# A two-layer decoder trunk on one core: seven weight pieces per pair of k-tiles from the first pair on, ten begun products in sections, and x's first tile loaded ahead of the weights

## The chip, the cores and the metric

The kernel runs on one core of one Trainium2 chip. The metric is device time in microseconds for one execution, the median of several runs. A core has five engines that run side by side, each through its own list of instructions in order: TensorE (PE in the profile; PEld is its weight load), VectorE (DVE), ScalarE (ACT), GpSimd (POOL) and SyncE (SP). Here SP issues the DMA transfers (SPq).

## The reference, cut to what matters

The trunk has two layers on 256 rows of 2048 values. Layer 0 is a Mamba-2 mixer, layer 1 an attention layer. The change touches layer 0 alone, up to its scan:

```python
shift, scale, gate = split(silu(c) @ ada_w[0] + ada_b[0], 3)
h = x * (1 + scale) + shift                       # 256 x 2048
z, xBC, dt = split(h @ in_w)                      # in_w: 2048 x 10304
xBC = silu(causal_depthwise_conv(xBC) + conv_b)   # -> xs, B, C
y = ssd_scan(xs * softplus(dt), -exp(A_log), B, C) + xs * D
y = rmsnorm_per_group(y * silu(z)) @ out_w
x = layer_norm(alpha * x + (1 + gate) * y)
```

Everything is computed in f32. The input `c` is one vector, so `silu(c) @ ada_w` is a product of a matrix with a vector.

## The kernel before, in words

**Tiles.** The 2048 values of the contraction are 16 k-tiles of 128. The first product `h @ in_w` is cut into 20 blocks of 512 columns: `bc` blocks 0 to 3 (for head groups 0/1, 2/3, 4/5, 6/7; `win[0]` to `win[3]`), `xs` blocks for groups 0 to 7 (`win[4]` to `win[11]`) and `z` blocks for groups 0 to 7 (`win[12]` to `win[19]`). A block needs 8 *pieces*; a piece is the weights of two k-tiles, 128 x 1024 f32 (`raw`, L86). So layer 0's first product is 160 pieces.

**Precision.** Each f32 operand is split into a rounded high half and a rest. ACT writes the high half of a piece (`whi`, L94), DVE the low half (`wlo`, L96), and each product is three matmuls: high with high, high with low, low with high. A piece takes 24 matmuls of 256 columns where it is the stationary operand (`cm_piece`, `bc` and `xs`, L120 to L122) or 12 of 512 where it streams (`tm_piece`, `z`, L173 to L175). There are six buffers for `raw` and three each for `whi` and `wlo`.

**The modulation.** `ada_w[0]` is stored by columns of the output, as 128 x 2048 tiles (`araw`). One DVE instruction multiplies such a tile with `silu(c)`, which stands in every partition (`cb_`), and sums along the row (L239): one *dot product* gives scale or shift of one k-tile. So a k-tile of `h` needs two loads of 1 MB and two dot products, then `ada_bias` (L244), the modulation on ACT (`htmp`, L381), the high half on ACT (`actT`, L382) and the low half on DVE (L383). `h_step` (L366) is one such dot product with what follows; `fetch` (L361) loads the next column, at most four ahead. `xt` holds two k-tiles of the transposed x.

**The first phase** (L354 to L452) runs while `h` comes into being. The two blocks `win[0]` and `win[4]` are computed whole, piece by piece as the k-tiles appear, in PSUM banks of their own. PE would have little to do in that time, so other products are *begun*: the table `begun` (L295) names the block, the k-tile at which its first part ends, and a place in SBUF. The sum up to there is copied from PSUM to that place by ACT (L443). Here eight products are begun, with 34 of their pieces, one product after the other. The list `order` has 50 pieces. In the first two pairs of k-tiles it has four pieces, in the later ones seven, and at the end the small product for `dt` comes with two loads (L411). `fetch_piece` (L398) loads a piece some places ahead of its use.

**Behind it**, `product` (L329) computes each remaining block from its k-tile `k0` on, and adds the part in SBUF, where there is one: on DVE (L340 for `z`, L347 for the others). The group's convolution (DVE, L308) and scan (`stage1`, `stage2`) follow; DVE's share of the scan is L513 to L553. The 16 dot products of layer 0's gate are put in one per five pieces (`background`).

**The order.** The program is written in one order, and a scheduler of the language orders it anew on each engine by its own estimate of when things are ready. Every load goes through SP in order; a load whose buffer is not free yet holds up those behind it.

## Time and profile before

| what | value |
|---|---|
| median of 3 runs | 1313.19 us (1312.98 to 1313.73) |
| the profiled execution | 1312.58 us, its span 1310.8 us |
| PE busy | 1241.7 us (95%) |
| DVE busy | 1027.8 us (78%) |
| ACT busy | 704.7 us (54%) |
| mean DMA rate over the span | 256 GB/s |
| first matmul | 20.6 us |

Read it in stretches, since the share of busy time is a mean over stages with different limits. The first phase ends at about 185 us, the scan of layer 0 at about 540. A matmul's end is modelled, so busy PE time also holds stretches in which PE runs below its best pace; counts of pieces per time tell more.

### The profile page before, as it was taken

What the parts mean: (1) busy time and instruction counts of PE and PEld (TensorE: products, weight loads), DVE (VectorE), ACT (ScalarE), POOL (GpSimd) and SP (SyncE); (2) the same over time, 40 slices, a digit from 0 to 9 for tenths busy, and PEclk for the clock granted to TensorE, in tenths of its full rate; (3) what the DMA queues carried; (4) which work ended last, traced back from release to release, by engine and by line L of the source; (5) the groups of instructions that cost most, each with busy time, mean ns of one, the idle gap of its engine ahead of it and who ended that gap; (6) DMA issues with size and microseconds to landing.
All of it is one profiled execution on the core that took longest, in us unless ns stands there. A gap on an engine that the chain in (4) does not pass through costs nothing.

```text
span 1310.8 us, 19308 instructions
## 1 busy us (share of the span) xinstructions
PE 1241.7 (95%) x7378; PEld 1091.6 (83%) x7378; DVE 1027.8 (78%) x1447; ACT 704.7 (54%) x1028; POOL 26.4 (2%) x20
## 2 busy tenths in 40 slices
PE   3799999999999999999999899999999999999995
PEld 3699988899989899767888699888888888888884
DVE  6889786999996688889765577888787757758677
ACT  3454478757766677864333444444445644444551
POOL 0000000000000000000000043000000000000000
PEclk9999999999999999999999999999999999999998
DMA  9999867777857555388977675899998664363571
GB/s 386 423 422 423 303 218 250 266 265 275 306 200 233 177 192 177 123 294 322 384 258 219 194 225 181 302 406 339 351 391 309 212 187 151 100 191 96 160 273 65
DMA packets 80446, 335.86 MB, mean 256 GB/s; under 512 B 8961, under 2 KB 9057, under 8 KB 67553
## 3 DMA queue, kind: packets, MB, share of 16 engines
q1 hardware_dynamic: 80352, 334.62, 71.8%
q8 instruction: 58, 0.95, 0.3%
q14 instruction: 36, 0.29, 0.1%
HBM read 332.41 MB, written 2.18 MB: 255 GB/s over the span
## 4 chain that ended last, share of the span: by engine, by line
PE 77%; DVE 10%; DMA 6%; ACT 4%; issue 3%; SPq 0%; ACTq 0%; DVEq 0%
PE acc L152 11%; PE acc L174 11%; PE acc L175 11%; PE acc L173 11%; PE acc L122 7%; PE acc L120 7%; PE acc L121 7%; PE acc L153 6%; DMA araw<-in_ada 5%; DVE wlo L96 3%; DVE araw L239 2%; PE py L551 2%; DVE cacc L308 1%; ACT whi L94 1%; PE aux L755 1%
## 5 line engine op out<-in xcount | busy, mean ns | idle before, releaser
L96 DVE TENSOR_TENSOR wlo<-raw,whi 128x1024 fp32r<-128x1024 f32 x394 | 484.5, 1239 | 198.9 <-ACT whi L94 193.1
L94 ACT ACTIVATE whi<-raw 128x1024 fp32r<-128x1024 f32 x394 | 414.5, 1057 | 374.9 <-PE acc L175 174.2
L173 PE MATMUL acc<-whi,actT 128*128 128x512 f32 x704 | 271.6, 394 | 22.8 <-ACT actT L382 20.6
L174 PE MATMUL acc<-wlo,actT 128*128 128x512 f32 x704 | 277.1, 394 | 4.8 <-DVE wlo L96 4.6
L120 PE MATMUL acc<-actT,whi 128*128 128x256 f32 x960 | 272.6, 287 | 6.2 <-ACT whi L94 4.7
L122 PE MATMUL acc<-actT,wlo 128*128 128x256 f32 x960 | 269.8, 286 | 5.1 <-DVE wlo L96 5.0
L121 PE MATMUL acc<-actT,whi 128*128 128x256 f32 x960 | 271.6, 284 | 0.0
L152 PE MATMUL acc<-actT,whi 128*128 128x512 f32 x704 | 250.1, 397 | 0.0
L239 DVE SCALAR_TENSOR_TENSOR araw<-araw,cb__72 128x2048 f32<-128x2048 f32 x96 | 219.3, 2285 | 14.8 <-DMA araw<-in_ada 14.5
L153 PE MATMUL acc<-actT,wlo 128*128 128x256 f32 x704 | 201.3, 286 | 0.9 <-DVE wlo L96 0.9
L120 PEld LDWEIGHTS acc<-actT,whi 128*128 128x128 f32 x960 | 185.6, 194 | 8.3 <-ACT whi L94 5.9
L122 PEld LDWEIGHTS acc<-actT,wlo 128*128 128x128 f32 x960 | 183.6, 193 | 7.2 <-DVE wlo L96 7.2
L121 PEld LDWEIGHTS acc<-actT,whi 128*128 128x128 f32 x960 | 185.6, 193 | 0.4
L175 PE MATMUL acc<-whi,actT 128*128 128x512 f32 x448 | 175.1, 391 | 0.0
L173 PEld LDWEIGHTS acc<-whi,actT 128*128 128x128 f32 x704 | 132.0, 188 | 50.8 <-ACT actT L382 20.6
L174 PEld LDWEIGHTS acc<-wlo,actT 128*128 128x128 f32 x704 | 132.5, 188 | 35.8 <-DVE wlo L96 9.2
L152 PEld LDWEIGHTS acc<-actT,whi 128*128 128x128 f32 x704 | 132.1, 188 | 29.3
L153 PEld LDWEIGHTS acc<-actT,wlo 128*128 128x128 f32 x704 | 133.2, 189 | 2.4 <-DVE wlo L96 1.7
L175 PE MATMUL acc<-whi,ylo 128*128 128x512 f32 x256 | 100.5, 393 | 0.0
L175 PEld LDWEIGHTS acc<-whi,actT 128*128 128x128 f32 x448 | 84.4, 188 | 16.8
L175 PEld LDWEIGHTS acc<-whi,ylo 128*128 128x128 f32 x256 | 48.0, 188 | 9.6
L308 DVE SCALAR_TENSOR_TENSOR cacc<-acc,prm,cacc 128x253 f32<-128x253 f32 (+2 forms) x96 | 42.1, 474 | 7.9 <-ACT cacc L305 7.5
(203 smaller groups left out, 1064.7 us busy)
## 6 DMA issues: line engine op xcount, KB each, us to landing
araw<-in_ada SPq DMA_DIRECT2D x96, 1024.0 KB, 7.6
raw<-in_win SPq DMA_DIRECT2D x160, 512.0 KB, 5.0
raw<-in_wkv SPq DMA_DIRECT2D x72, 512.0 KB, 6.4
raw<-in_wout SPq DMA_DIRECT2D x64, 512.0 KB, 4.7
raw<-in_wbin SPq DMA_DIRECT2D x64, 512.0 KB, 3.6
raw<-in_wk SPq DMA_DIRECT2D x24, 512.0 KB, 8.0
cbc<-cumd SPq DMA_DIRECT2D x16, 512.0 KB, 5.3
raw<-in_wbout SPq DMA_DIRECT2D x16, 512.0 KB, 4.5
```

The costliest lines, as they stand in the source:

```text
L94: S.activation(hi, raw, AF.Copy)
L96: latest[0] = V.tensor_tensor(lo, raw, hi.bitcast(F32), op=ALU.subtract)
L120: T.matmul(o, hi[:, k, c_], ahi[:, kt, :], start=first, stop=False, skip_group_check=True)
L121: T.matmul(o, hi[:, k, c_], alo[:, kt, :], start=False, stop=False, skip_group_check=True)
L122: T.matmul(o, lo[:, k, c_], ahi[:, kt, :], start=False, stop=kt == k1 - 1, skip_group_check=True)
L152: T.matmul(ps[n], hi[:, k, c_], xp[:, kt], start=kt == 0, stop=False, skip_group_check=True)
L153: T.matmul(ps[n][:, 0, :], lo[:, k, c_], xhi[:, kt, :], start=False, stop=kt == KT - 1, skip_group_check=True)
L173: T.matmul(ps[b], h_, hi[:, k, :], start=kt == k0, stop=False)
L174: T.matmul(ps[b], h_, lo[:, k, :], start=False, stop=False)
L175: T.matmul(ps[b], l_, hi[:, k, :], start=False, stop=kt == k1 - 1)
L239: V.scalar_tensor_tensor(raw, raw, 1.0, cb_, op0=ALU.mult, op1=ALU.mult, accum_out=mod[layer][:, ct, j:j + 1])
L308: V.scalar_tensor_tensor(acc[:, o:], ps[:, :L - o], w[:, j:j + 1], acc[:, o:], op0=ALU.mult, op1=ALU.add)
```

## The change

Four things change, all in the first phase.

- Ten products are begun instead of eight, with 40 pieces instead of 34. `z4` and `z5` are new. The parts end at other k-tiles: z0 6 (was 4), z1 4 (6), bc2 4 (8), z2 14 (10), bc4 12 (10), z6 10 (14); xs1 and bc6 keep 4 and 12.
- Each pair of k-tiles has seven pieces from the first on: two of the whole blocks (`h` in the table of rows) and five of begun products. The list has 56 pieces.
- A begun product may be done in *sections*. A dot behind a piece in the table ends a section; its sum leaves PSUM then. The first section of a product is copied by ACT, a later one is added by DVE to what lies in SBUF. bc4, bc6 and z2 have two sections, the other seven products one.
- The loads at the start stand in another order, and `prm` (the small parameters) with its addition of 1.0 comes behind x's first tile.

Behind the phase nothing is edited, but `product` finds other parts: z4 has 5 pieces left instead of 8, z5 has 4 instead of 8, and both now add their part on DVE.

```diff
-    nc.sync.dma_start(prm, par)
...
-    V.tensor_scalar(adab[:, :, :, 1:3], adab[:, :, :, 1:3], 1.0, None, op0=ALU.add)
...
-            begun = {("z", 0): (win[12], 4, szt[0]), ("xs", 1): (win[5], 4, as_cm(y[0])),
-                     ("z", 1): (win[13], 6, szt[1]), ("bc", 2): (win[1], 8, as_cm(y[1])),
-                     ("z", 2): (win[14], 10, y[2]), ("bc", 4): (win[2], 10, as_cm(y[3])),
-                     ("bc", 6): (win[3], 12, as_cm(y[5])), ("z", 6): (win[18], 14, y[6])}
+            begun = {("z", 0): (win[12], 6, szt[0]), ("z", 1): (win[13], 4, szt[1]),
+                     ("xs", 1): (win[5], 4, as_cm(y[0])), ("bc", 2): (win[1], 4, as_cm(y[1])),
+                     ("z", 2): (win[14], 14, y[2]), ("bc", 4): (win[2], 12, as_cm(y[3])), ("z", 4): (win[16], 6, y[4]),
+                     ("bc", 6): (win[3], 12, as_cm(y[5])), ("z", 6): (win[18], 10, y[6]), ("z", 5): (win[17], 8, y[7])}
...
+                for row in ("b4:0. b6:0. h z2:0. b2:0 x1:0 h", "b2:1. x1:1. z1:0 z1:1. z4:0 h h",
+                            "z4:1 z4:2. z0:0 z0:1 z0:2. h h", "z5:0 z5:1 z5:2 z5:3. z6:0 h h",
+                            "z6:1 z6:2 z6:3 z6:4. b4:1 h h", "b4:2 b4:3 b4:4 b4:5. b6:1 h h",
+                            "b6:2 b6:3 b6:4 b6:5. z2:1 h h", "h h z2:2 z2:3 z2:4 z2:5 z2:6."):
...
-                for i in range(3):
-                    fetch()
+                fetch()
+                fetch()
+                fetch_x(0)
+                nc.sync.dma_start(prm, par)
+                V.tensor_scalar(adab[:, :, :, 1:3], adab[:, :, :, 1:3], 1.0, None, op0=ALU.add)
+                fetch_piece()
+                fetch_piece()
+                fetch()
+                fetch_piece()
+                for _ in range(2):
+                    for _ in range(2):
+                        h_step()
+                    while late:
+                        late.pop()()
                     fetch_piece()
-                for _ in range(4):
-                    h_step()
-                while late:
-                    late.pop()()
...
+                    if ends:
+                        del begin[k]
                         for w in range(2):
-                            S.activation(part[k][2][:, w, :] if z else part[k][2][:, 2 * w:2 * w + 2, :],
-                                         pss[k][w], AF.Copy)
-
-                    n = (i + 1) if i < 8 else 8 + (i - 7) * 4 / 7
-                    while h_step.i < min(len(cols), 4 + int(n)):
+                            place = part[k][1][:, w, :] if z else part[k][1][:, 2 * w:2 * w + 2, :]
+                            if k in done:
+                                V.tensor_tensor(place, pss[k][w], place, op=ALU.add)
+                            else:
+                                S.activation(place, pss[k][w], AF.Copy)
+                        done.add(k)
+
+                    while h_step.i < min(len(cols), 4 + (i + 1) * 4 // 7):
                         h_step()
```

**SP's queue at the start.** Each row is a load: its line, the tile it fills, its source, its size. `cb_` is c in every partition, `prm` the parameters, `araw` an ada column, `raw` a weight piece, `xt` two k-tiles of x. Before:

```order
L63 DMA cb__72<-in_c 128x2048
L70 DMA prm<-in_par 128x529
L232 DMA araw<-in_ada 128x2048
L88 DMA raw<-in_win 128x1024
L232 DMA araw<-in_ada 128x2048
L88 DMA raw<-in_win 128x1024
L232 DMA araw<-in_ada 128x2048
L88 DMA raw<-in_win 128x1024
L373 DMA xt<-in_xT 128x512
L232 DMA araw<-in_ada 128x2048 x4
L88 DMA raw<-in_win 128x1024
L373 DMA xt<-in_xT 128x512
```

Now:

```order
L63 DMA cb__72<-in_c 128x2048
L230 DMA araw<-in_ada 128x2048 x2
L366 DMA xt<-in_xT 128x512
L415 DMA prm<-in_par 128x529
L87 DMA raw<-in_win 128x1024 x2
L230 DMA araw<-in_ada 128x2048
L87 DMA raw<-in_win 128x1024
L230 DMA araw<-in_ada 128x2048 x2
L87 DMA raw<-in_win 128x1024
L230 DMA araw<-in_ada 128x2048 x2
L87 DMA raw<-in_win 128x1024 x3
L366 DMA xt<-in_xT 128x512
```

x's first tile stood behind three columns and three pieces, and stands behind two columns now. Up to x's second tile there are seven columns in both; the pieces are seven instead of four.

**DVE's list at the start**, from the first dot product on (L239, now L237). L244 (L242) is the bias, L383 (L384) the low half of `h`, L96 (L95) the low half of a piece. Before:

```order
L239 SCALAR_TENSOR_TENSOR araw,mod_84<-araw,cb__72 128x2048
L96 TENSOR_TENSOR wlo<-raw,whi 128x1024
L239 SCALAR_TENSOR_TENSOR araw,mod_84<-araw,cb__72 128x2048
L244 TENSOR_TENSOR mod_84<-mod_84,prm 128x2
L96 TENSOR_TENSOR wlo<-raw,whi 128x1024
L239 SCALAR_TENSOR_TENSOR araw,mod_84<-araw,cb__72 128x2048
L96 TENSOR_TENSOR wlo<-raw,whi 128x1024
L383 TENSOR_TENSOR actT<-htmp,actT 128x256
L239 SCALAR_TENSOR_TENSOR araw,mod_84<-araw,cb__72 128x2048
L244 TENSOR_TENSOR mod_84<-mod_84,prm 128x2
L239 SCALAR_TENSOR_TENSOR araw,mod_84<-araw,cb__72 128x2048
L383 TENSOR_TENSOR actT<-htmp,actT 128x256
```

Now:

```order
L237 SCALAR_TENSOR_TENSOR araw,mod_83<-araw,cb__72 128x2048 x2
L416 TENSOR_SCALAR prm<-prm 128x32x2
L242 TENSOR_TENSOR mod_83<-mod_83,prm 128x2
L384 TENSOR_TENSOR actT<-htmp,actT 128x256
L95 TENSOR_TENSOR wlo<-raw,whi 128x1024 x2
L237 SCALAR_TENSOR_TENSOR araw,mod_83<-araw,cb__72 128x2048
L95 TENSOR_TENSOR wlo<-raw,whi 128x1024
L237 SCALAR_TENSOR_TENSOR araw,mod_83<-araw,cb__72 128x2048
L242 TENSOR_TENSOR mod_83<-mod_83,prm 128x2
L237 SCALAR_TENSOR_TENSOR araw,mod_83<-araw,cb__72 128x2048
L384 TENSOR_TENSOR actT<-htmp,actT 128x256
```

The first k-tile's low half stood behind three dot products and three splits, and stands behind two dot products now. The second one stands behind the fifth dot product in both.

**DVE's list in the sixth pair of k-tiles**, where the second section of bc4 ends (`y_94` is its place). Only the changed kernel has the rows at L466:

```order
L95 TENSOR_TENSOR wlo<-raw,whi 128x1024 x2
L237 SCALAR_TENSOR_TENSOR araw,mod_83<-araw,cb__72 128x2048
L466 TENSOR_TENSOR y_94<-acc,y_94 128x512
L242 TENSOR_TENSOR mod_83<-mod_83,prm 128x2
L466 TENSOR_TENSOR y_94<-acc,y_94 128x512
L95 TENSOR_TENSOR wlo<-raw,whi 128x1024
```

Two additions have come in between the dot products and the splits of the weights.

41 lines of the change are left out of this document (24 added, 17 removed).

## The prediction, made before the result was known

> **What bounds the kernel now.** I read the page first, then the time cut into stretches, then the waits of the matmul engine (PE). The first table has one row for a stretch: its ends in us, its length, the busy time (and instructions) of PE, PE's weight loads, VectorE (DVE), ScalarE (ACT) and GpSimd, the granted clock, the DMA share, GB/s.
>
> ```profile
> 0.00:21.00 21.00, 0.40 (x1) 0.41 (x2) 11.39 (x14) 7.38 (x7) 0.20 (x4) 1.00 0.93 366
> 21.00:70.00 49.00, 38.93 (x227) 32.37 (x227) 42.53 (x48) 20.14 (x29) 0.00 (x0) 1.00 1.02 423
> 70.00:140.00 70.00, 70.00 (x532) 67.55 (x531) 64.00 (x68) 36.42 (x47) 0.00 (x0) 1.00 1.02 422
> 140.00:185.00 45.00, 43.56 (x288) 39.49 (x288) 33.37 (x50) 27.13 (x38) 0.00 (x0) 1.00 0.71 243
> 185.00:240.00 55.00, 53.74 (x325) 46.81 (x324) 41.11 (x67) 40.87 (x70) 0.00 (x0) 1.00 0.63 218
> 240.00:400.00 160.00, 156.96 (x1090) 145.62 (x1089) 152.29 (x230) 112.78 (x186) 0.00 (x0) 0.99 0.78 272
> 400.00:540.00 140.00, 138.15 (x966) 127.59 (x965) 106.77 (x189) 100.42 (x169) 0.00 (x0) 1.00 0.54 172
> ```
>
> PE is the bound almost everywhere; nearly all of its large holes lie before 70 us. It does nothing for 20.6 us, and from 21 to 70 it is busy for 38.9 of 49 us while the DMA runs at 423 GB/s: there the loads set the pace. From 70 to 140 the loads run as fast and PE is full. What ended the early holes, in total us, times, longest:
>
> ```profile
> PE acc L173 <- ACT actT L382: 20.6, 1, 20.6
> PE acc L120 <- ACT whi L94: 4.7, 4, 1.6
> PE acc L174 <- DVE wlo L96: 2.7, 4, 0.8
> PE acc L122 <- DVE wlo L96: 2.3, 5, 0.5
> ```
>
> First the modulated input, then splits of weight pieces that had not landed. The second thing to see is in the stretch 240 to 400: DVE is busy for 152.3 of 160 us there, so a gain for PE alone does not carry through it unhindered.
>
> **The unit of work.** The loads of x's tiles by SP mark a pair of k-tiles. Once seven pieces come with each pair, PE is full and the marks show its pace; the third row counts DVE's splits before 66 us, the fourth is the last early wait of PE.
>
> ```profile
> 73.14 0.42 SPq L373 DMA_DIRECT2D xt<-in_xT  x1
> 132.66 0.42 SPq L373 DMA_DIRECT2D xt<-in_xT  x1
> 0.00:66.00 66.00, 13.47 (x11) 1.00 0.99 405
> 67.73 0.39 PE L122 MATMUL acc<-actT,wlo 128*128 128x256 f32 x1 [0.52 <-DVE wlo L96]
> ```
>
> Three pairs take 59.52 us, 19.84 a pair, 2.834 us a piece. Before 66 us 11 pieces were split. At 67.73 the 12th, which waits for its low half, has run 4 of its 24 matmuls. So PE has then done 11.17 pieces, 31.7 us of work, and has lost 36.1 us. From there it runs full to 140 and beyond. The sum is made of lost time: all matmuls are the same in both kernels, only where PE waits differs.
>
> **The start, step by step.** Each row: start, duration, engine, line, instruction, and in brackets the idle time before it with what ended it.
>
> ```profile
> 5.56 1.91 ACT L68 ACTIVATE cb__72<-cb__72 128x2048 f32<-128x2048 f32 x1 [3.55 <-DMA cb__72<-in_c]
> 9.32 2.29 DVE L239 SCALAR_TENSOR_TENSOR araw<-araw,cb__72 128x2048 f32<-128x2048 f32 x1 [2.38 <-DMA araw<-in_ada]
> 10.47 1.06 ACT L94 ACTIVATE whi<-raw 128x1024 fp32r<-128x1024 f32 x1 [3.00 <-DMA raw<-in_win]
> 14.14 1.06 ACT L94 ACTIVATE whi<-raw 128x1024 fp32r<-128x1024 f32 x1 [2.62 <-DMA raw<-in_win]
> 19.50 0.60 ACT L381 ACTIVATE htmp<-xt,mod 128x256 f32<-128x256 f32 x1 [0.57 <-DMA xt<-in_xT]
> 20.60 0.79 PE L173 MATMUL acc<-whi,actT 128*128 128x512 f32 x1 [20.60 <-ACT actT L382]
> 22.04 0.63 PE L173 MATMUL acc<-whi,actT 128*128 128x512 f32 x1
> 22.47 0.63 PE L174 MATMUL acc<-wlo,actT 128*128 128x512 f32 x1
> 26.35 0.40 PE L173 MATMUL acc<-whi,actT 128*128 128x512 f32 x1
> 26.58 0.40 PE L174 MATMUL acc<-wlo,actT 128*128 128x512 f32 x1
> 26.68 0.42 DVE L383 TENSOR_TENSOR actT<-htmp,actT 128x256 fp32r<-128x256 f32 x1
> 30.63 1.06 ACT L94 ACTIVATE whi<-raw 128x1024 fp32r<-128x1024 f32 x1 [5.08 <-DMA raw<-in_win]
> ```
>
> By size, c is 1.049 MB, an ada column 1.049, prm 0.271, a weight piece 0.524, an x tile 0.262. In issue order the first piece is complete at 2.89 MB (10.47 us), the second at 4.47 MB (14.14), the fourth at 11.02 MB (30.63): 0.43 MB/us at first, then 2.52 us per MB. Now the order is c, two columns, x, prm, two pieces. The second column is complete at 3.15 MB, about 11.1 us. Its dot product takes 2.29 to 13.4. From the start of the modulation to the matmul it is 1.1 us (19.50 to 20.60), with the bias ahead of it that makes 14.7; then the first split, of a piece that landed at 13.5 (4.20 MB), takes 1.06: the first matmul runs at about 15.8 instead of 20.6. That alone is worth little, since the second k-tile needs the fourth column (7.35 MB, 21.4 us) and its low half stands behind a fifth dot product on DVE, to about 26.8; it was complete at 27.1 before (the row at 26.68), so nothing is gained there.
>
> What counts is when the seven pieces of the first pair are through. The seventh is complete at 12.59 MB, by the slope 34.6 us. The durations of the steady stretch are in this view (busy us, mean ns, then idle before and what ended it):
>
> ```profile
> L239 DVE SCALAR_TENSOR_TENSOR araw<-araw,cb__72 128x2048 f32<-128x2048 f32 x15 | 34.3, 2284 | 0.0
> L96 DVE TENSOR_TENSOR wlo<-raw,whi 128x1024 fp32r<-128x1024 f32 x25 | 30.1, 1223 | 5.8 <-ACT whi L94 5.6
> L94 ACT ACTIVATE whi<-raw 128x1024 fp32r<-128x1024 f32 x25 | 25.6, 1050 | 10.9 <-PE acc L121 10.0 <-ACT whi L94 0.9
> L443 ACT ACTIVATE y<-acc 128x512 f32<-128x512 f32 x6 | 3.6, 598 | 12.4 <-PE acc L122 8.2 <-PE acc L175 3.8
> L383 DVE TENSOR_TENSOR actT<-htmp,actT 128x256 fp32r<-128x256 f32 x7 | 3.0, 422 | 0.0
> L239 DVE DVE_READ_ACCUMULATOR araw<-araw,cb__72 128x1 f32 x14 | 1.2, 82 | 0.0
> ```
>
> DVE must do seven dot products (7 x 2.37), seven splits (7 x 1.22) and three low halves of the input with small ones (1.9 in all) from about 8.7 us on (the first column now stands 0.27 MB earlier than at 9.32): it is through at 35.8 us without a wait. I add 3 us of waits, for the first modulation and for splits that stand on ACT behind the copies of sections of one piece (L443 is such a copy, 0.60 us; the first four begun pairs of banks are each evicted after one piece or two). That gives 38.8. The last piece's matmuls begin after the sixth piece's, and end at about 42.5. Ends: 39.7 if only the landing counts (34.6 + 1.06 + 1.22 + 2.83), 45 if the waits double. Work done is then 7 pieces, 19.84 us, so 22.7 us are lost instead of 36.1: **-13.4 us** (-16.2 to -10.9).
>
> PE's spacing is 0.43 us at 22.0 and 0.23 at 26.4, a ratio of 1.9: it starts slow and is at full pace some us later. The new start works in short bursts. If PE were still slow at the second k-tile, 30 matmuls of 0.118 us (2.834 / 24) behind 26.8 us would take 6.6 instead of 3.5 us, and with four pieces behind them pair 0 would end at 26.8 + 6.6 + 11.3 = 44.7, 2.2 us later; the total would be 1306.5. The longest of the later holes in the waits above is 1.6 us, and the pairs behind them ran at 2.834 us a piece, so I keep the sum and make this a rival. [...]
>
> **The other seven pairs.** DVE's row sums for a pair are 4 x 2.37 + 7 x 1.22 + 1.2 = 19.2 us at most; in the stretch 70 to 140, where just this was done, it was busy for 64.0 of 70 us and PE had no hole. New are the sections' additions: b4, b6 and z2 are added to what lies in SBUF, 6 additions of 0.68 us (priced below), and 4 more copies on ACT of 0.60, hidden under matmuls (ACT 36.4 of 70). Without that cover they cost 6.5. The loads need 8.13 MB a pair, 19.3 us at 422 GB/s, against PE's 19.84: hidden, with little to spare. The 1.4 us of hole after 140 (43.56 of 45) stay. Ends: 0, and +6.9 if DVE's 19.2 and the waits in its row (5.8 us over 25 splits, 1.6 a pair) do not overlap. I take **+1.5**, near the measured stretch.
>
> **Behind the first phase.** Six pieces fewer remain (z4 and z5 lose seven, z2 two, b4 and z0 one each; b2 and z6 gain two, z1 one). PE's work moves, the total is the same. But DVE gets four additions more (z4, z5), and the scan's work of one more head group falls among the 49 splits of the stretch that was 240 to 400:
>
> ```profile
> L96 DVE TENSOR_TENSOR wlo<-raw,whi 128x1024 fp32r<-128x1024 f32 x49 | 59.1, 1216 | 1.9 <-ACT whi L94 1.9
> L239 DVE SCALAR_TENSOR_TENSOR araw<-araw,cb__72 128x2048 f32<-128x2048 f32 x16 | 36.5, 2283 | 1.4 <-DMA araw<-in_ada 1.4
> L513 DVE TENSOR_TENSOR seg<-seg,cb 128x1024 f32<-128x1024 f32 x6 | 7.2, 1216 | 0.0
> L526 DVE TENSOR_TENSOR y<-aux,prm 128x512 f32<-128x512 f32 x6 | 4.1, 678 | 0.0
> L340 DVE TENSOR_TENSOR y<-acc,y 128x512 f32<-128x512 f32 x2 | 1.4, 682 | 0.0
> ```
>
> A group is 2 x 1.22 (seg) and 11 operations of 0.68 us like L526: 9.9 us on DVE, at most; PE's matmuls for it are some 4.5 us (160 us less 49 x 2.834 and the 3 us of holes leave 18 for three to four groups). So PE would need 163 us, DVE 152.3 + 9 = 161. If DVE keeps its 7.7 us of idle time it takes 169: +6. If it fills up, 0; nothing excludes a small gain elsewhere, since fewer splits stand behind 400. I take **+2.5**, and **+0.5** (0 to 2) for groups 4 and 5, where fewer matmuls now cover the chain of the scan; from 400 to 540 DVE has room (106.8 of 140).
>
> **Sum.** -13.4 + 1.5 + 2.5 + 0.5 = -8.9. The profiled execution took 1312.6 us (span 1310.8): 1303.7. The median of the runs is 0.6 above it: **1304.3**. By the terms' ends, not all at once, the forecast's own range is 1298.5 to 1308.5.
>
> **Rivals.**
> - DVE takes most of it back: both later terms at their upper ends, +6 behind the phase and +4 in it. For it: 95% of DVE in 240 to 400. Against: at 95% PE still had only 3 us of holes (156.96 of 160). -13.4 + 10 = -3.4: 1309.8. Chance 0.20.
> - Half clock after the new start, as above: 1306.5. Chance 0.10.
> - The loads bound it, so that it doesn't do what it says: 3.1 MB more before the phase ends. If the queue gave 380 GB/s, a pair would take 21.4 us, +1.6 x 7 = +11: 1311.9, no change that can be told. Against: 422 GB/s for 140 us without a dip. Chance 0.07.
> - Slower: DVE paces the seven pairs. At 19.2 + 1.6 us a pair, plus the six additions, that costs 6.9 + 4.1 = 11, and with +6 behind it the sum is +3.6: 1316.8. It decides from 21.8 us a pair on its own. Against it: these pairs already ran at 19.84. Chance 0.08.
>
> **The numbers.** The forecast keeps 0.55. A measurement tells about 0.2%, 2.6 us, from no change. Faster: 0.55 + 0.10 + most of 0.20 = 0.82; same 0.10; slower 0.08. Range 1298.5 to 1311: the forecast's ends, and upward the first rival whole and part of the third.
>
> **What would show it.** Right: first matmul at 15 to 17 us; the seventh split by 40; no wait of PE over 1 us between 45 and 140; marks of x's tiles 19.8 to 20.2 apart; the first product behind the phase at about 190 (42.5, 49 pieces and the dt product's two at 2.834, 1.4 and 1.5). Wrong: PE waits on low halves all through the first phase (DVE paces), marks over 21 us apart, a second half-pace stretch behind 25 us, or a gain of 12 us at 190 that is under 6 at 540.

## The result, and the profile after

The changed kernel takes 1326.66 us (median of four runs, 1321.5 to 1327.8), the kernel before beside it 1313.09 (1309.93 to 1313.73). The ratio is 1.0101, 95% interval 1.0069 to 1.0132: slower by 1.0%, where 1304.3 and faster was forecast; no rival went so far (1316.8 was the slowest). The profiled execution of the changed kernel is the shortest of the four, 1321.5 us with a span of 1319.6; it shows 8.9 us of loss against that of before. What the other runs lose beyond it, some 5 us, has no profile.

The same stretches as in the prediction (ends, length, PE, PEld, DVE, ACT, POOL, clock, DMA share, GB/s), now of the changed kernel:

```profile
0.00:21.00 21.00, 5.54 (x28) 5.04 (x28) 11.01 (x14) 7.27 (x7) 0.20 (x4) 1.00 0.90 360
21.00:70.00 49.00, 44.87 (x286) 40.67 (x287) 41.80 (x45) 26.08 (x38) 0.00 (x0) 0.97 1.02 422
70.00:140.00 70.00, 66.39 (x416) 59.21 (x415) 60.69 (x65) 35.33 (x46) 0.00 (x0) 1.00 1.01 415
140.00:185.00 45.00, 37.28 (x282) 35.53 (x281) 36.52 (x48) 19.96 (x29) 0.00 (x0) 0.94 0.63 227
185.00:240.00 55.00, 54.16 (x325) 47.89 (x325) 37.75 (x58) 39.98 (x59) 0.00 (x0) 0.99 0.77 263
240.00:400.00 160.00, 153.32 (x1090) 143.41 (x1089) 151.41 (x230) 112.26 (x181) 0.00 (x0) 0.99 0.74 264
400.00:540.00 140.00, 137.29 (x972) 127.34 (x970) 110.59 (x193) 101.74 (x176) 0.00 (x0) 1.00 0.54 170
```

Up to 70 us PE is busy for 11.1 us more than before (5.54 + 44.87 against 0.40 + 38.93). Then it loses 3.6 us from 70 to 140, 6.3 from 140 to 185, 3.6 from 240 to 400.

**Lead at equal work.** PE's matmuls are the same in all kernels here but stand in another order, so I add them up at one fixed spacing each (0.2345 us for 512 columns, 0.1185 for 256, 0.062 for 128, 0.05 for 64) and compare the times at which a sum is reached. "Work" below is this sum in us. The table is worked out from the traces, a row for each kernel of this document; minus is ahead of the kernel before.

```
work done (us)         40    140    150    250    320    440    470   1100
before, at (us)      76.2  178.6  188.6  301.1  374.1  506.3  542.4 1202.6
changed kernel      -12.0   -7.0   +2.4   -3.8   +5.5   +5.7  +11.3   +8.9
own dt buffer       -12.2   -7.2   +0.5   -3.4   +6.5   +7.4  +13.4  +13.3
three ahead         -11.6   -9.9   -9.7   -9.5   -0.2   +0.1   +5.6   +5.5
dt last             -11.9   -7.0   -7.1   -5.0   +4.9   +4.5  +10.3   +8.3
new loads only       +0.6   +0.6   +0.6   -0.2   -0.2   -0.5   -0.5   +0.0
three, stage1(6)    -11.4   -9.7   -9.5  -10.4   -1.1   +1.0   -0.8   -0.2
... gate late       -12.2  -10.5  -10.3   -9.3   +4.8   +4.9   +1.5   +0.3
... splits ahead    -10.8   -9.1   -3.5   -5.9   -3.7   +3.8   +2.1   +4.7
... z2 three left   -11.9   -9.8   -9.6   -5.3   -0.5   +8.8   +6.9   +4.6
before, no gate      +0.8   +0.8   +0.8   +1.6   +1.1   +1.2   +1.2  +42.6
three, no gate      -11.2   -8.0   -7.9   -9.3   -3.3   -4.4   +1.7  +43.4
before, 4+4 buffers  +0.5   +5.4   +5.1   +6.5   +6.7   +4.4   +2.0   +4.6
before, stage1(6)    -0.4   -0.4   -0.4   -1.5   -1.3   +3.7   +2.4   +2.4
same begun, dt 4    -11.7   -3.7   -4.0   -4.5   -4.5   -4.5   -4.4   -5.4
same begun, dt 6    -11.7   -7.8   -8.1   -5.4   -5.4   -5.2   -5.1   -6.0
same, old loads     -11.6   -1.8   -2.1   -1.9   -1.9   -1.7   -1.6   -4.1
xs7 three           -12.1   -8.2   -8.0   -6.3   -4.0   -5.9   -0.7   -3.5
xs7 three, stage1   -11.6   -7.7   -7.5   -8.9   -6.5   -8.3   +0.6   -2.7
xs7 five, stage1    -11.5   -9.9   -9.4  -11.4   -8.8  -12.3   +3.2   +1.5
```

The spacings for 128 and 64 columns are smaller than most of theirs in the trace: in the kernel before the medians of the four widths are 0.227, 0.120, 0.109 and 0.112 us. With these medians the entries up to work 150 and at 1100 move by 1 us at most, those from 250 to 470, where the scan's small matmuls stand, by up to some 3 us. A difference of 2 or 3 us there says nothing.

So the gain came, 12.0 us at 76 us, and was lost in four places: 5 us in the rest of the first phase, 9.4 at `dt`'s product (work 140 to 150), 9.3 in groups 1 to 3 of the scan (250 to 320), 5.6 at groups 6 and 7 (440 to 470). Between 150 and 250 6.2 us came back, behind 470 2.4; that leaves the 8.9. The 9.3 run from a peak of the lead to a trough (7.2 with the median spacings): from 150, behind `dt`, to 320 it is 3.1. With three pieces ahead, where nothing comes back in between, it is 9.5. PE's waits of the changed kernel show the last three and a part of the first; the rows are of 70 to 140, of 140 to 190 and of 190 to 560 us:

```profile
PE acc L119 <- ACT whi L93: 1.8, 2, 1.6
...
PE acc L436 <- ACT whi L93: 5.5, 2, 5.3
...
PE acc L121 <- DVE wlo L95: 7.6, 4, 2.9
PE aux L545 <- DVE ms L580: 4.9, 1, 4.9
```

**The hole at `dt`.** PE's row, then ACT's, then SP's of the changed kernel (L436 is `dt`'s first matmul; L303 and L308 are the convolution of group 0; L87 is any load into a `raw` buffer):

```profile
181.76 0.58 PE L436 MATMUL acc<-actT,whi 128*128 128x256 f32 x1 [5.28 <-ACT whi L93]
...
172.92 0.56 ACT L303 ACTIVATE cacc<-acc,prm 128x256 f32<-128x256 f32 x1 [1.88 <-PE acc L121]
175.12 1.28 ACT L308 ACT_TABLE_LOAD   x1 [1.63 <-DVE cacc L306]
179.51 0.81 ACT L308 ACTIVATE bcm<-cacc 128x256 f32<-128x256 f32 x2 [1.78 <-DVE cacc L306]
180.67 1.04 ACT L93 ACTIVATE whi<-raw 128x1024 fp32r<-128x1024 f32 x1
186.54 2.96 ACT L93 ACTIVATE whi<-raw 128x1024 fp32r<-128x1024 f32 x3 [0.33 <-DMA raw<-in_wdt]
...
150.00 20.50 SPq L87 DMA_DIRECT2D raw<-in_win  x7
170.55 0.42 SPq L449 DMA_DIRECT2D cc<-in_cst  x1
172.33 10.99 SPq L87 DMA_DIRECT2D raw<-in_wdt  x2
```

SP's last seven pieces go out as buffers come free, 2.9 us apart, and `dt`'s loads stand behind all of them: with five pieces ahead the whole list has been asked for when the program comes to `dt`. Five of the six `raw` buffers then hold pieces that are used only behind `dt`. So the first of its loads goes out at 172.33 and the second at 183.0, when DVE is done with the first. The first landed 4.0 us behind its issue, but ACT's split for it stands at 180.67, behind the convolution of group 0, which waits for PE once and for DVE twice. The hole is 5.3 of the 9.4 us; the rest is shorter waits and matmuls at a lower clock behind it (0.72 from 182 to 190). The kernel before issued both loads at 157:

```profile
155.28 0.42 SPq L430 DMA_DIRECT2D cc<-in_cst  x1
157.02 1.46 SPq L88 DMA_DIRECT2D raw<-in_wdt  x2
```

**The holes in the scan.** DVE's rows before the longest wait on a low half (group 3), PE's row behind it, and PE's row at group 7:

```profile
369.70 0.69 DVE L345 TENSOR_TENSOR y<-acc,y 128x512 f32<-128x512 f32 x1 [2.06 <-PE acc L121]
370.31 2.28 DVE L237 SCALAR_TENSOR_TENSOR araw<-araw,cb__72 128x2048 f32<-128x2048 f32 x1
373.25 0.48 DVE L306 SCALAR_TENSOR_TENSOR cacc<-y,prm,cacc 128x255 f32<-128x255 f32 x1
...
376.04 0.48 DVE L306 SCALAR_TENSOR_TENSOR cacc<-y,prm,cacc 128x255 f32<-128x255 f32 x1
376.43 0.16 DVE L213 SCALAR_TENSOR_TENSOR ay<-at,ay 128x2 f32<-128x2 f32 x1
376.50 1.23 DVE L95 TENSOR_TENSOR wlo<-raw,whi 128x1024 fp32r<-128x1024 f32 x1
...
377.78 0.58 PE L121 MATMUL acc<-actT,wlo 128*128 128x256 f32 x1 [2.94 <-DVE wlo L95]
...
544.73 0.52 PE L545 MATMUL aux<-cc,xs 128*128 128x128 f32 x2 [4.85 <-DVE ms L580]
```

The low half at 376.50 stands behind a dot product and two short chains that DVE does by turns, the convolution (L306) and the reciprocal root (L213 is its last step), from 372.5 on. At 377.78 the transposes of `stage1` are done and the next matmul is the one that needs this half. In the other two long waits of this kind (1.8 us at 266, 1.7 at 317) the low half stands behind other work: two dot products at 266, the convolution and additions of the scan at 317. At 544.73 PE stands in the transposes of group 7 until group 6's reciprocal root is through, with five pieces of z7 behind them in its list.

### The profile page after: what moved, and what is told of

It reads as the page before. It is cut to its first block, busy times and chain, and to the rows that moved or that the text cites. A ratio compares the mean times of both kernels' runs of the same rounds, so it can differ in the third digit from the quotient of the medians.

```text
span 1319.6 us, 19301 instructions
## 1 busy us (share of the span) xinstructions
PE 1245.2 (94%) x7378; PEld 1096.0 (83%) x7378; DVE 1033.3 (78%) x1457; ACT 707.5 (54%) x1032; POOL 26.4 (2%) x20
## 4 chain that ended last, share of the span: by engine, by line
PE 78%; DVE 10%; ACT 5%; DMA 4%; issue 3%; SPq 0%; DVEq 0%; ACTq 0%
PE acc L151 12%; PE acc L173 11%; PE acc L174 11%; PE acc L172 11%; PE acc L121 7%; PE acc L119 7%; PE acc L120 7%; PE acc L152 6%; DMA araw<-in_ada 3%; DVE wlo L95 3%; DVE araw L237 2%; PE py L575 2%; ACT whi L93 2%; PE aux L779 1%; DMA raw<-in_win 1%
## 5 line engine op out<-in xcount | busy, mean ns | idle before, releaser
L95 DVE TENSOR_TENSOR wlo<-raw,whi 128x1024 fp32r<-128x1024 f32 x394 | 484.9, 1241 | 204.7 <-ACT whi L93 203.3
L237 DVE SCALAR_TENSOR_TENSOR araw<-araw,cb__72 128x2048 f32<-128x2048 f32 x96 | 219.6, 2287 | 14.7 <-DMA araw<-in_ada 14.2
L306 DVE SCALAR_TENSOR_TENSOR cacc<-acc,prm,cacc 128x255 f32<-128x255 f32 (+2 forms) x96 | 42.8, 479 | 9.9 <-ACT cacc L303 9.5
```

Of the source, the lines that this page charges most:

```text
L95: latest[0] = V.tensor_tensor(lo, raw, hi.bitcast(F32), op=ALU.subtract)
L237: V.scalar_tensor_tensor(raw, raw, 1.0, cb_, op0=ALU.mult, op1=ALU.mult, accum_out=mod[layer][:, ct, j:j + 1])
L306: V.scalar_tensor_tensor(acc[:, o:], ps[:, :L - o], w[:, j:j + 1], acc[:, o:], op0=ALU.mult, op1=ALU.add)
```

## Experiments

### Where the 9.4 us at `dt` come from

**Own buffer for `dt`.** Its two loads go into a free buffer of the ada columns, in one go.

```diff
+                    wd = wp1.tile([P, D], F32, name="araw", bufs=2)
+                    for q in range(2):
+                        nc.sync.dma_start(wd[:, 1024 * q:1024 * q + 1024], wdt[q])
...
-                                  for t in split(load_piece(wdt[q])))
+                                  for t in split(wd[:, 1024 * q:1024 * q + 1024]))
```

> The changed kernel with one edit: the two loads of dt's weights go into an ada column's buffer, which is free by then, instead of two of the six buffers for weight pieces. Theory A (shared buffers): in the changed kernel five of the six buffers hold pieces that come behind the dt product, the second dt load can only be issued once the first one is split (172.3 and 183.0 us), and PE loses 9.4 us between 171 and 191 by equal matmul work. Then that loss goes: after the first phase this kernel is 7 to 10 us ahead of the kernel before by equal matmul work, and the median falls from 1326.7 to 1316 to 1320. Theory B (VectorE and ScalarE order pace the phase, the dt loads only show it): the wait moves to the next split, at most 3 us are won, 1323 to 1327.

1327.84 us, ratio 1.0119 (1.0098 to 1.0141). The second load no longer waits, and the hole stays:

```profile
170.82 0.90 SPq L433 DMA_DIRECT2D araw<-in_wdt  x2
...
179.93 1.04 ACT L93 ACTIVATE whi<-araw 128x1024 fp32r<-128x1024 f32 x1
...
181.02 0.58 PE L439 MATMUL acc<-actT,whi 128*128 128x256 f32 x1 [4.76 <-ACT whi L93]
```

Both loads go out at 170.8 and 171.3, behind the seven pieces. ACT's splits of them, at 179.93 and 181.33, end no wait for a load; the first comes behind the convolution all the same. The table gives 1.9 us less at work 150, and no time is won in the end. So the missing buffer alone is not it: at the end PE waits for the place of the split in ACT's list. The next run asks whether the late issue puts it there.

**Three pieces ahead.** The start fetches three pieces ahead instead of five.

```diff
                     while late:
                         late.pop()()
-                    fetch_piece()
```

> The changed kernel with three pieces loaded ahead instead of five (as in the kernel before), so that the ring has room for dt's two loads. Theory A: the hole before the dt product goes, as in the kernel with its own buffer; the start loses up to 2 us, since the sixth and seventh pieces are issued later: 1317 to 1321. Theory B: no difference at the end of the phase, and the start gets worse: 1326 to 1330.

1318.28 us, ratio 1.0045 (1.003 to 1.006). SP issues the loads together, eight us earlier:

```profile
162.61 0.43 SPq L448 DMA_DIRECT2D cc<-in_cst  x1
164.38 1.46 SPq L87 DMA_DIRECT2D raw<-in_wdt  x2
...
170.46 1.05 ACT L93 ACTIVATE whi<-raw 128x1024 fp32r<-128x1024 f32 x1
```

ACT splits the first at 170.46, between parts of the convolution, and the lead at work 150 is 9.7 us instead of -2.4. One line took out the whole hole. What it changes is the time of the issue and, with it, the place of the split in ACT's list; no run changes one without the other.

**`dt` last.** With five ahead, `dt`'s product comes behind the last piece.

```diff
-                    if i == len(order) - 5:
-                        nc.sync.dma_start(cc, cst)
-                        dt_product()
...
+                nc.sync.dma_start(cc, cst)
+                dt_product()
                 bc_conv(0, tiles(first[0]))
```

> The changed kernel with the dt product written behind the list of pieces instead of five places ahead of its end. Theory A: dt's loads now find buffers as the ring turns, the hole of 5.4 us and what follows it go: 7 to 10 us ahead of the kernel before at equal matmul work behind the phase, 1316 to 1320; the chain behind dt (softplus, cumulated sums) starts some 14 us later and may cost up to 3 of it before the first scan. Theory B: at most 3 us, 1323 to 1327.

1326.33 us, ratio 1.0094 (1.007 to 1.0118), not the 1316 to 1320 of theory A. The lead at work 150 is 7.1 us, so this too removes the hole; but by 250 the three kernels with `dt` late are within 1.6 us of each other (-3.8, -3.4, -5.0), probably since the scan cannot begin before `dt` is through. What else is missed at the end lies behind.

**The new order of the first loads alone**, in the kernel before: two columns, x's tile, parameters, two pieces, with its own 34 begun pieces and four pieces a pair at the start.

```diff
-                for i in range(3):
-                    fetch()
-                    fetch_piece()
+                fetch()
+                fetch()
+                fetch_x(0)
+                nc.sync.dma_start(prm, par)
...
+                fetch_piece()
+                fetch_piece()
+                fetch()
+                fetch_piece()
```

> The kernel before with only the new order of the first loads (x's first tile and then the parameters behind two ada columns, ahead of the weight pieces); eight begun products, three pieces ahead, four pieces in the first pairs. If the early matmul by itself is worth nothing, as the prediction said, since the second k-tile's columns and the loads pace the stretch to 70 us: first matmul near 16 us, the lost time at 70 us within 2 us of the kernel before, 1311 to 1315. Rival: the start as such brings most of the gain of the changed kernel's first 64 us (12 us): 1301 to 1305.

1312.46 us, ratio 0.9994 (0.9983 to 1.0005), no change. PE starts at 15.4 us and waits elsewhere.

### What the scan loses

**stage1(6) ahead of xs7**, on three pieces ahead.

```diff
             for g in range(G - 1):
...
+                if g == G - 2:
+                    stage3(g - 1, rs)
+                    st1 = stage1(g)
                 product("xs", g + 1)
-                if rs is not None:
-                    stage3(g - 1, rs)
-                st1 = stage1(g)
+                if g < G - 2:
+                    if rs is not None:
+                        stage3(g - 1, rs)
+                    st1 = stage1(g)
```

> Three pieces ahead as in the run before, and in group 6 the first stage of the scan (stage1) is written ahead of the product of xs7 instead of behind it. Theory C (in PE's list all of group 6 and group 7 stands behind xs7, at two pieces of z7, so that the transposes of group 7 wait 5.1 us for VectorE's reciprocal root of group 6): the hole at about 534 to 539 us and the half-pace matmuls behind it go, some 6.8 us, so 1310 to 1313, and the lead at 320 units of matmul work stays where it was without the edit. Rival (the chain of the last two groups is simply longer than the work that is left to cover it): the hole moves by a piece or two, 1316 to 1319.

1311.92 us, ratio 0.9995 (0.9984 to 1.0007). As expected: the wait on `ms` is gone from PE's waits (240 to 560 us), the rest is as it was.

```profile
PE acc L121 <- DVE wlo L95: 7.6, 4, 2.9
PE acc L119 <- ACT whi L93: 1.4, 1, 1.4
PE aux L544 <- ACT xs L308: 0.8, 1, 0.8
```

**The control**, the same move in the kernel before:

> The kernel before with stage1(6) written ahead of the product of xs7, and nothing else. Theory C: its list has group 6 ahead of xs7 already and the hole that the changed kernel has at group 7 is not in it, so 1311 to 1314. Rival (the old place costs both kernels, and the edit is a gain of its own): 1308 to 1310.

1314.8 us, ratio 1.0009 (0.9998 to 1.0019): worth nothing there, and the table shows 5 us lost between 320 and 440. The hole belongs to the changed kernel.

**Gate dot products later**, on the run with stage1(6) moved.

```diff
             for g in range(G - 1):
+                R = (1, 9) if g < 3 else (1, 4)
```

> As the run with stage1(6) moved, and the 16 gate dot products of layer 0 come one in nine pieces in groups 1 and 2 and one in four from group 3 on, instead of one in five throughout. Theory D (from 235 to 340 us VectorE is full, 93 percent and more, and a group now has fewer pieces over it, so its work sets the pace): some three dot products fewer there, 7 us of VectorE, give back 4 to 7 of the 9 us that are lost between 250 and 320 units of matmul work: 1304 to 1308 if the run without this edit gives 1311. Rival (single waits behind the order of VectorE's list, not its amount of work): within 2 us of the run without this edit, or slower where the dots are now denser.

1314.81 us, ratio 1.002 (1.001 to 1.003): the theory of DVE's amount of work falls in this form. With fewer dot products the wait on low halves grew, and one hole became 4.4 us (240 to 560 us):

```profile
PE acc L121 <- DVE wlo L95: 9.1, 3, 4.4
```

**No gate dot products**, in the kernel before and on three pieces ahead. The gate's column is set to zero instead; 16 loads and 16 dot products are left out.

```diff
-                    queue(wp1, [(0, "gate", kt) for kt in range(KT)])
+                    V.memset(mod[0][:, :, 2:3], 0.0)
```

> The kernel before without the 16 gate dot products of layer 0: the gate column is set to zero, so 16 loads and 38 us of VectorE (16 x 2.37) are left out. It is the base line for the next run. PE's holes from 240 to 540 us were 5 us in all, so at most that is gained: 1308 to 1313.

> The changed kernel with three pieces ahead and without the same 16 gate dot products. Theory D (VectorE's amount of work makes the loss between 250 and 320 units of matmul work): the lead over the kernel before without them stays at 7 us or more at 320 units, then the hole of group 7 takes some 7: 3 us below to 1 us above the base line. Rival (the order of the lists): the lead is gone by 320 units as with the dot products, and the time is 4 to 7 us above the base line.

1356.71 and 1353.84 us. Both are 40 us longer from about 860 us on, where loads of layer 1 now come in pairs and PE waits for weights; I did not follow that, so only the scan of these two is read. Against the kernel before without them, the lead falls from 10.9 us at 250 to 4.4 at 320, a loss of 6.5 where it is 9.3 with them, stays there to 440 (5.6), and the hole of group 7 comes as before. DVE's load makes the loss larger, but with 38 us less of it two thirds remain, or somewhat under half if one counts from 150 on (4.3 of 9.5).

**One piece further ahead with the splits.** On stage1(6) moved, four pairs of `whi` and `wlo` and four `raw` instead of three and six (the space is the same).

```diff
-        raw = wp.tile([P, 1024], F32, name="raw", bufs=6)
+        raw = wp.tile([P, 1024], F32, name="raw", bufs=4)
...
-        hi, lo = into or [wp.tile([P, 1024], F32R, name=n) for n in ("whi", "wlo")]
+        hi, lo = into or [wp.tile([P, 1024], F32R, name=n, bufs=4) for n in ("whi", "wlo")]
```

> The run with three pieces ahead and stage1(6) moved, and the buffers of the split weights go from three pairs to four, those of the raw pieces from six to four (the space is the same). Theory F (the holes at 308 and 368 us are low halves that stand on VectorE behind 5 to 10 us of convolution, scan and reciprocal-root work; with one more pair the split may run one piece, 2.8 us, earlier): of the 9 us lost between 250 and 320 units of matmul work at least 5 return: 1303 to 1308. Rival G (VectorE has too much work there, and being ahead does not help when it is full): 1310 to 1313. If four raw buffers are too few, SP's transfers show waits in the first phase and it takes 1314 and more.

1314.36 us, ratio 1.0006 (0.9993 to 1.0019), no better than without the edit. The long waits on low halves shrink from 7.6 to 5.4 us, and between 250 and 320 only 2.2 us are lost. But 5.6 are lost at 150 already, and 7.5 between 320 and 440.

**The same buffers in the kernel before:**

> The kernel before with four pairs of split buffers and four raw buffers. PE's holes in it from 240 to 540 us are under 5 us together, so it can gain 1 to 4: 1309 to 1312; in the start (68 us) the loads bound it, and nothing changes unless four raw buffers are too few, which gives 1315 and more.

1319.22 us, ratio 1.0039 (1.0023 to 1.0056), of which 4.9 us are lost between work 40 and 140.

**Other places for the same 40 pieces.** On stage1(6) moved, z2 has three pieces left as in the kernel before, z4 four and z5 three.

```diff
-                     ("z", 2): (win[14], 14, y[2]), ... ("z", 4): (win[16], 6, y[4]), ... ("z", 5): (win[17], 8, y[7])}
+                     ("z", 2): (win[14], 10, y[2]), ... ("z", 4): (win[16], 8, y[4]), ... ("z", 5): (win[17], 10, y[7])}
```

> The run with three pieces ahead and stage1(6) moved, and the same 40 begun pieces in other places: z2 five pieces begun as in the kernel before (three left for the scan of group 1), z4 four, z5 five. Theory H (the loss between 250 and 320 units comes from the two pieces of z2 that are missing there, 5.7 us of matmuls, while 340 to 400 units have room on VectorE, 13 of 20 us): 1305 to 1308. Rival (which low half is caught behind a burst is a matter of the list's order, and moving pieces moves the holes): 1310 to 1314.

1319.66 us, ratio 1.0041 (1.0026 to 1.0056): it falls. Between 250 and 320 it loses 4.8 us instead of 9.3. But it has lost 4.3 before that, between 150 and 250, where the run without the edit lost nothing, so that at 320 the two stand level (-0.5 and -1.1). Then it loses 9.3 more between 320 and 440, where z4 and z5 now have fewer pieces. PE's waits on low halves:

```profile
PE acc L121 <- DVE wlo L95: 9.0, 6, 3.5
```

So far each edit had moved the loss and none had removed it. What they share is that pieces are missing behind the first phase and that each has a new list.

### The start without the missing pieces

**The same 34 begun pieces.** The changed start (five others with the first two pairs, x's tile early, three ahead), but begun are the products and k-tiles of the kernel before; four others come with each of the other pairs.

```diff
+                for r, row in enumerate(("b4:0. b6:0. h z2:0. z0:0 x1:0 h", "z0:1. x1:1. z1:0 z1:1 b2:0 h h",
+                                         "z1:2. b2:1 b2:2 z6:0 h h", "b2:3. z6:1 z6:2 z6:3 h h",
+                                         "z6:4 b4:1 b4:2 b4:3 h h", "z6:5 b4:4. b6:1 b6:2 h h",
+                                         "z6:6. b6:3 b6:4 b6:5. h h", "h h z2:1 z2:2 z2:3 z2:4.")):
+                    words = row.split()
+                    pace += [4 + 4 * r + 4 * (j + 1) // len(words) for j in range(len(words))]
...
-                    if i == len(order) - 5:
+                    if i == len(order) - 4:
...
-                    while h_step.i < min(len(cols), 4 + (i + 1) * 4 // 7):
+                    while h_step.i < min(len(cols), pace[i]):
```

> The change's start (seven pieces with the first two pairs, x's first tile ahead of the weights, three pieces ahead), but only the 34 begun pieces of the kernel before, so that six instead of seven pieces come with each of the other six pairs; dt's product stands ahead of the last four. Behind the first phase the lists of PE and the amount of work are those of the kernel before. Theory L (the loss of the scan comes from the six pieces that are missing there and the other list that follows, not from the earlier start): a lead of 8 to 12 us at 150 units of matmul work stays within 3 us to the end, 1301 to 1306. Rival M (the scan has a pace of its own on VectorE from 235 us on, so whatever arrives earlier waits there): the lead is under 3 us at 320 units, 1310 to 1314. Six pieces a pair take PE 17.0 us and the loads 17.4 at 422 GB/s, so 2 to 3 of the 12 us may go in the first phase itself.

1307.87 us, ratio 0.9966 (0.9953 to 0.998), faster than both kernels, by 0.3% than the one before. The lead of 4.5 us at 250 is 4.5 at 320, at 440, and 4.4 at 470: the scan loses nothing. The earlier start is not what costs there. The first phase took more than expected, 11.7 to 3.7. A pair with six pieces takes 17.9 us by the marks of x's tiles (77.92 to 131.75 in three steps, read in the next run): its 7.60 MB need 18.0 at the 422 GB/s of 70 to 140 us there, not the 17.4 of the expectation, against PE's 17.0. And PE waits 3.5 us at `dt`.

**`dt` two pieces earlier**, `len(order) - 6` in the same place:

> As the run with the 34 begun pieces of the kernel before, with dt's product two pieces earlier (ahead of the last two pieces of the first products instead of behind them). If the chain behind dt (split, product, softplus) is what PE waits for between the phase and the scan, 1 to 3 us less than that run; otherwise within 1.5 us of it.

1307.32 us, ratio 0.9954 (0.9937 to 0.9971). In the profile 0.9 us more lead stays through the scan; the medians do not tell the two apart. Its stretches and its waits in 240 to 560 us, beside those of the changed kernel above:

```profile
240.00:400.00 160.00, 157.42 (x1096) 145.50 (x1095) 152.50 (x236) 113.98 (x186) 0.00 (x0) 1.00 0.78 272
400.00:540.00 140.00, 138.09 (x970) 127.63 (x969) 107.08 (x185) 101.02 (x166) 0.00 (x0) 1.00 0.53 168
...
PE acc L121 <- DVE wlo L95: 2.0, 4, 0.7
```

DVE is as full as ever (152.5 of 160) and PE has 2.6 us of holes. A full DVE is not by itself a loss for PE; it depends on what stands ahead of a low half when PE comes to it.

**With the old order of loads** at the start (on the run with `dt` four ahead), the first matmul is at 20.5 us again:

> As the run with the 34 begun pieces of the kernel before, with the first loads in the order of the kernel before (parameters first, x's first tile behind three columns and three pieces). The first matmul then runs at 20 to 21 us instead of 16. If the seven pieces of the first pair are bound by loads and VectorE, as the prediction has it, the seventh piece ends only 0 to 2 us later and the time is within 2 us of that run; if the early first matmul carries the gain, 4 to 5 us more.

1309.73 us, ratio 0.9978 (0.9968 to 0.9988). The lead at work 40 is 11.6 us with either order: up to there all of the gain is the seven pieces, as the prediction had it. At work 140 the old order has 1.9 us less, as by the medians; the two ratios are not told apart.

### Amount or place

**Three and five pieces of xs7**, on the run with `dt` six ahead: more is begun, but only from the last `xs` product, so that what is written for groups 1 to 5 is still that of the kernel before. The third run and the second have stage1(6) moved as well.

```diff
+                     ("xs", 7): (win[11], 6, as_cm(y[7]))}
...
-"z0:1. x1:1. z1:0 z1:1 b2:0 h h", "z1:2. b2:1 b2:2 z6:0 h h", "b2:3. z6:1 z6:2 z6:3 h h", "z6:4 b4:1 b4:2 b4:3 h h",
+"z0:1. x1:1. z1:0 z1:1 x7:0 h h", "z1:2. x7:1 x7:2. b2:0 b2:1 h h", "b2:2 b2:3. z6:0 z6:1 z6:2 h h", "z6:3 z6:4 b4:1 b4:2 b4:3 h h",
```

> As the run with the 34 begun pieces and dt's product six pieces ahead of the end, with three more begun: of xs7, which is needed last, behind 430 us, where VectorE is busy for 107 of 140 us. Five others come with each of the first five pairs, four with the last three. PE's list for groups 1 to 5 is still that of the kernel before. Theory L (cover and list of groups 1 to 5 carry the 9 us): the lead of 9 to 10 us at 150 units stays within 3 us to 430; the three pieces are missing behind xs6, where groups 6 and 7 then stand closer together, 1 to 4 us: 1303 to 1307. Rival (any piece taken out of the scan costs its share, 15 us for six, so 7 for three): 1309 to 1312.

1307.75 us, ratio 0.9955 (0.9943 to 0.9967).

> As the run with three begun pieces of xs7, with stage1(6) ahead of xs7. If the closer groups 6 and 7 cost something there, it comes back as in the run with three pieces ahead: 1302 to 1305, 1 to 4 us under that run. If not, within 2 us of it, or up to 4 slower as in the kernel before with this edit, which was 1.3 slower.

1311.67 us, ratio 0.9987 (0.9979 to 0.9996): with three pieces gone the move does harm, 3.9 us by the medians, 0.8 by the profiled spans (1308.1 against 1307.3).

> As the run before, with five begun pieces of xs7 instead of three, five others with every pair but the last, which has four. Theory L: the first phase keeps 1 us more of its lead, groups 1 to 5 stay as they are, groups 6 and 7 lose 3 to 7: 1303 to 1309. Rival (any piece costs its share): 1313 to 1316.

1314.0 us, ratio 1.0004 (0.9994 to 1.0014), above the 1303 to 1309 expected and in the range of the rival, that any piece costs its share. With five pieces missing the lead is 11.4 us at 250, 8.8 at 320 and 12.3 at 440: groups 1 to 5 lose nothing in sum. Then 15.5 are lost up to 470, between 500 and 540 us:

```profile
500.00:540.00 40.00, 30.91 (x194) 26.88 (x192) 35.75 (x78) 35.65 (x73) 0.00 (x0) 0.87 0.26 80
...
PE aux L547 <- ACT xs L308: 4.4, 2, 4.0
PE acc L173 <- DVE wlo L95: 2.6, 1, 2.6
PE acc L121 <- DVE wlo L95: 2.0, 1, 2.0
```

Five pieces are 14.2 us of matmuls (2.834 each), and about that is lost just where they are missing (15.5, or 12.5 with the median spacings): the work of groups 6 and 7 on ACT and DVE takes its time, and there is less to do meanwhile. Three missing cost 5.2 us between 440 and 470, of their 8.5, and 8.9 with stage1(6) moved; by 1100 the losses behind 440 are 2.4, 5.6 and, with five missing, 13.8. So in these two groups the rival comes near. But the share is not the same at every place: in the changed kernel seven pieces, 19.8 us, are missing in z4 and z5, and between 320 and 440, where DVE adds their parts, it loses 0.2 us; counted from another place it is up to 4.

For the loss up to work 320 neither the two missing pieces of z2 nor any other single thing is shown to be the cause: each edit moved the loss, and it went only where the begun pieces of the kernel before, and with them its whole list, came back. Of the runs above three are level at the top, the two with these begun pieces and the early loads, and the one with three pieces of xs7.

## Why the prediction was wrong

The terms of the prediction and what came in their place, as losses of the lead on the clock of the kernel before, worked out like the table above. The stretches behind the first phase depend on the spacings (with the medians +7.3, +3.1, +7.5 and -2.7):

| stretch | said | came |
|---|---|---|
| the start | -13.4 | -12.0 |
| the other seven pairs, to 179 us | +1.5 | +5.0 |
| 179 to 240, with `dt` | 0 | +5.3 |
| 240 to 400 | +2.5 | +4.0 |
| 400 to 540 | +0.5 | +9.5 |
| behind | 0 | -2.9 |

- **The start, -13.4 us (-16.2 to -10.9): right, -12.0.** First matmul at 15.39 us (15 to 17 said), seven low halves by 40, the work of seven pieces done at 42.9 (42.5 said). That the early first matmul "alone is worth little" holds: no change alone, and the lead at work 40 is the same without it. The pieces per pair carry the gain.
- **The other seven pairs, +1.5 (0 to 6.9): +5.0, in the range.** Some 3 us of it go around one hole at 80 us, where ACT's split stands behind the copy of a section that waits for PE, as the prediction had it for the first pair only:

```profile
78.19 1.28 ACT L468 ACTIVATE sz<-acc 128x512 f32<-128x512 f32 x2 [5.86 <-PE acc L174]
79.37 2.00 ACT L93 ACTIVATE whi<-raw 128x1024 fp32r<-128x1024 f32 x2
80.47 0.38 PE L119 MATMUL acc<-actT,whi 128*128 128x256 f32 x1 [1.63 <-ACT whi L93]
```

  "No wait of PE over 1 us between 45 and 140" fails here, and again at 139.5, where PE waits 1.4 us for a low half (once more at 161). x's tiles came 21.0 us apart (43.09 to 148.26 in five steps), not 19.8 to 20.2, and at the bound that was set for being wrong. The cost of one wait was set at nothing by the cover of the matmuls, without asking which copy stands ahead of which split.
- **`dt`: a term that is missing, +9.4 at once, 5.7 of it left at 250 and 3.4 at the end** (against three ahead). The step that failed is "The 1.4 us of hole after 140 (43.56 of 45) stay". The diff shows two more pieces fetched ahead, and the prediction counted the loads in MB and never asked what stands ahead of `dt`'s loads: five ahead in six buffers put them behind the whole list, with one buffer left for the two, and ACT's split for them behind the convolution. Three pieces ahead shows it, with one line.
- **240 to 400, +2.5 (0 to +6): +4.0, in the range, but by luck.** The reason given, the sum of busy times, is not what happened: 161 against 163 us would have fitted, and DVE's busy share did not rise (151.4 of 160). What PE waited for was a low half behind other work in DVE's list, 6.4 us in three waits. A fourth pair of split buffers cut the loss between 250 and 320 to 2.2 and lost as much elsewhere; the begun pieces of the kernel before took it away at the same busy share of DVE. How much of it is missing pieces and how much the other list stays open.
- **400 to 540, +0.5 (0 to 2): +9.5, outside the range.** This is the second step that failed: the term is for groups 4 and 5 alone, and "from 400 to 540 DVE has room (106.8 of 140)" is true and was no help. 5.6 us were lost in groups 6 and 7, which are in none of the terms: PE waited there for the end of one chain, and stage1(6) ahead of xs7 takes that wait away. What the two groups of the term lost is 0.2 from work 320 on, 3.4 from 400 us on (2.0 with the median spacings), so near its range.
- **The rivals.** "DVE takes most of it back" has 10 us at most, where 5.0 were lost in the seven pairs and 13.5 from 240 to 540. The slower rival (DVE paces the seven pairs) is not what happened: PE's waits on low halves in 70 to 140 are 1.7 us in all. Half pace at the second k-tile did come, 1 us behind a hole of 2.5 us: from 26.1 to 29.5 us the clock is 0.50, and from 27.07 to 29.41 the matmuls stand 0.21 us apart, then 0.12.

```profile
27.07 0.41 PE L121 MATMUL acc<-actT,wlo 128*128 128x256 f32 x1
27.28 0.41 PE L119 MATMUL acc<-actT,whi 128*128 128x256 f32 x1
```

  These 2.3 us cost about 1 us, half of the 2.2 that this rival has; the lead at 76 us is inside the forecast range with it. The loads carried 415 to 422 GB/s, as assumed.
- **Two sums.** The third rival's 1311.9 does not come out of its terms: -13.4 + 11 + 2.5 + 0.5 is +0.6, 1313.8. PE's 163 us in 240 to 400 is 161.5 by the text (157.0 busy and 4.5 more), no more than DVE's 161. Neither would have changed the forecast's sign.
- The sign that was to prove it wrong, a gain of 12 us at 190 that is under 6 at 540, was near: the gain was 12 at 76, and gone at 190.

Where nothing is taken from the scan, with the begun pieces of the kernel before, the start is worth 5.2 us by the medians (1307.3 against 1312.5), not the 8.9 of the forecast: some of its 12 us goes again in the first phase.

## What to carry to other kernels

When work is moved ahead in time, ask of each place that it is taken from what it was covering there: a busy share of 95% says nothing on whether the cover was needed, and a chain on other engines can cost as much as the missing cover was long (in groups 6 and 7), or much less (in groups 4 and 5). Count buffers as well as bytes when a prefetch goes deeper, and look for the load with another purpose that stands in the same ring of buffers and the same queue. And where a list is in balance, any edit of it or of its buffers may cost some microseconds (the kernel before lost 5.8 us by other buffers alone), so an edit has to be run with its control.

## What the runs showed of the hardware

- **Behind holes of 1.8 to 2.9 us PE ran at half pace in some places and at full pace in others; the length of the hole did not settle it.** The same wait of 2.94 us, at the same place of the program, once with half pace behind it (stage1(6) moved: the clock is 0.50 for two us, eight matmuls, 0.21 us apart) and once without (gate late: 17 matmuls at 1.00, 0.12 us apart):

```profile
371.19 0.58 PE L121 MATMUL acc<-actT,wlo 128*128 128x256 f32 x1 [2.94 <-DVE wlo L95]
371.00:373.00 2.00, 1.81 (x8) 1.81 (x9) 2.00 (x7) 1.98 (x7) 0.00 (x0) 0.50 0.49 139
...
377.89 0.39 PE L121 MATMUL acc<-actT,wlo 128*128 128x256 f32 x1 [2.94 <-DVE wlo L95]
378.00:380.00 2.00, 2.00 (x17) 2.00 (x18) 2.00 (x6) 1.98 (x6) 0.00 (x0) 1.00 0.56 113
```

  In the traces of the kernel before and the changed kernel the clock stayed at 1.00 behind every hole of 0.7 to 1.7 us that stands alone. Behind the four of 4.85 to 5.73 us it was 0.50 for 3.4 to 6.9 us more. Between them it went either way: 1.00 behind 1.79 us (changed kernel, 266.45), but 0.50 for 3.4 us after 1.76 (kernel before, from 250.0, 1.3 us behind the hole), after 2.46 and after 2.94 (changed kernel, from 26.1 and 377.7). What decides between the two is not shown.
- Leaving out 16 loads and dot products of layer 0 made the kernel 40 us longer (42.6 and 43.4 at work 1100), hundreds of us later, where PE waited for weights: from 860 to 920 us PE is busy for 40.3 of 60 us in the kernel before without them, 59.9 with them. No run shows what moved the loads there.
